# Layer 1's gate row in the weights' stream, low parts ahead of the last half sums, another order at the passage

## The chip, the cores and the metric

The kernel runs on one core of one Trainium2 chip. The metric is the device time of one execution in microseconds (us); lower is better. TensorE does the matmuls, VectorE and ScalarE the elementwise work, GpSimd (POOL) some additions and the transfers that accumulate, SyncE (SP) issues the other transfers.

## The reference, cut to what matters

One step of a backbone of two layers on 512 latent and 128 context tokens (640 in all), width 1024. Layer 0 mixes with attention and spatial gating, layer 1 with a pooling mixer. Behind each mixer stands a squared-ReLU MLP of width 4096, each sub-layer with a norm, a shift and a scale in front and a gate behind:

```python
x = x + g1 * mix
h = rms_norm(x, norm2_g[l]) * (1 + sc2) + sh2
x = x + g2 * squared_relu_mlp(h, w_ff1[l], w_ff2[l])
```

`squared_relu_mlp(h, w1, w2)` is `relu(h @ w1)**2 @ w2`. The shift, scale and gate rows come from a product of the conditioning vector with `w_mod`; latent and context tokens have rows of their own. The end is `rms_norm(x, final_g)`. Inputs and outputs are float32.

## The kernel before, in words

**Numbers.** Every large product is made of three matmuls in a fast float32 format: each operand is split into a high part (a rounding copy) and a low part (the rest), and high*high, high*low and low*high are summed (`mm3`, L823 to L825).

**Weights.** `Weights` is one stream of items in a fixed order. An item's loads go from SP into raw buffers (tag `raw`, five of them, `RAWB`); `pump` takes the next item: ScalarE makes the high part (L213), and either VectorE the low part by a subtraction (L223, `st.lo = vec`) or ScalarE a negated copy (L216) onto which GpSimd's queue adds the raw weight by an accumulating transfer (L220, `st.lo = None`). The result takes one of eight slots until `free`. With `lagging` set, the low part and the return of the raw buffer are put off to the next pump, to `lows` or to the item's use. Items with a `use` of their own make something else of the raw buffer. `caps` changes the number of raw buffers that loads may hold from a given item on.

**The order of work** is written by hand: what is issued to an engine's queue is done in that order. Generators (`bg`, `g0`, `g1`) yield after small steps, and `bg.step`, `TURNS` and `MID` say where they go on. A character of `TURNS` is one step: `0` is one step of `g0` (norm and h of the first token chunk of layer 1's MLP), `1` one of `g1` (the second chunk's pooling: norm, `hh`, windows, differences), `w` a pump with an accumulated low part, any other letter a pump with VectorE's low part. Entry 0 comes ahead of the MLP, entries 1 to 8 ahead of the eight input blocks of its first four column products (L1481 with L1786), entries 9 to 16 ahead of the squared ReLU of columns 0 to 7 (L1803).

**The passage from layer 0 to 1.** The last two blocks of layer 0's W2 run over the output columns d for both token chunks (L1835 to L1855); for the second chunk the pooling of the first (`pool_vec(0)`) goes on beside it. At d = 6 `tick0` makes the pool products of the first chunk (`pool_mm`, L2094), whose sums go into x (L1429) and are squared by ScalarE and added by VectorE (L729) for the norm of the first chunk (L740 to L684). Four pumps stand within these pool products and one behind each column from d = 6 on. Then layer 1's MLP begins with four columns at once for the first chunk (L823 to L825, `up_ps`); at column 6 the pool products of the second chunk follow. PSUM has six banks for all of these.

**Layer 1's MLP** takes blocks of 512 hidden columns. From block 2 on the up products of both chunks are made with seven half products instead of eight (`up7`, L1595): products 0 to 6 use half sums of weights (`w1s_use`, L576 to L583) and of h. The down products then have tokens on the output's rows (`down_t`, L1510), and their sums are kept per token tile t and column half q in the place of x, which was parked in memory as xT.

**The last block (b = 7).** `up7` runs for two pairs of hidden tiles; before the second, `gate_load` loads the row of the gate for the latent tokens (`G`, a raw buffer, L1691, L2020). In the second pair, `last_gate` (L2032) multiplies the kept sums of tiles 3, 2, 0 and 1 by the gate and adds the parked x by an accumulating transfer of GpSimd (L2033). Then come the down products in the order `LASTS` = 4, 3, 2, 0, 1: four halves start with two of four hidden tiles (`cut`), and are finished in turn. Tile 4 (context tokens) is summed (L1738), then gated with the second gate row (`gate_load(1)`); every other half is gated out of PSUM (L2042), added (L2043), squared by ScalarE (L2057) and multiplied by the final gain (L2059). `last_out` (L2061) makes the norm's factor, scales and stores, for the first three tiles together, then for tile 0 and tile 1; the last half of tile 1 is cut in two quarters (`TAIL`).

## Time and profile before

| what | us |
|---|---|
| median of 3 runs (lowest, highest) | 1285.55 (1285.2, 1286.9) |
| the profiled execution's own time | 1285.38 |
| its span, first to last instruction | 1283.6 |
| TensorE busy | 1247.0 (97%) |
| VectorE busy | 796.9 (62%) |
| ScalarE busy | 571.1 (44%) |
| GpSimd busy | 198.5 (15%) |
| mean granted TensorE clock | 0.988 |

The span is taken from the profiled execution; its own time is 1.8 us longer. All times in the rows below count from the span's start. In a row of a timeline the first number is the start and the second how long the instruction (or the group of so many in a row) took; consecutive instructions of one engine overlap a little, so that the distance between two starts in a full queue is shorter than the first one's time. What stands in brackets is the time that the engine stood idle before it and what ended that. PE is TensorE, DVE VectorE, ACT ScalarE. A granted clock of 1.00 is 2.4 GHz, 0.50 is 1.2 GHz.

### The profile page before, as it was taken

The numbers are of one execution on the slowest core, as the hardware profiler recorded it, in microseconds if no ns is written. First come the engines' busy times: TensorE is split into PE (matmuls) and PEld (weight loads), VectorE is DVE, ScalarE is ACT, GpSimd is POOL, SyncE is SP. The second block draws the span as 40 slices with busy tenths as digits, with TensorE's granted clock in tenths as the row PEclk, the third lists the DMA queues.
The fourth block names the chain that finished last, engine by engine and source line by source line (L and its number), as shares of the span: only waits on it lengthen the run. The fifth ranks groups of instructions, "written<-read, shape, count | busy, mean of one in ns | idle before, by whom it ended". The sixth has DMA issues, their size and how long they took to land. (4 is left out here: it accounts for less than half of the span.)

```text
span 1283.6 us, 19571 instructions
## 1 busy us (share of the span) xinstructions
PE 1247.0 (97%) x7744; PEld 1135.7 (88%) x7744; DVE 796.9 (62%) x1455; ACT 571.1 (44%) x1022; POOL 198.5 (15%) x181
## 2 busy tenths in 40 slices
PE   6999999999999999999999999899999999999986
PEld 4899975689999999999999999889898989989875
DVE  5753854554766566666666637775576556675667
ACT  4445654543554434334332424745444515445154
POOL 0010122212122221313131314210000000000030
PEclk9999999999999999999999999899999999999988
DMA  7752696250344443535353441904113343132273
GB/s 297 262 167 68 152 254 235 97 197 1 120 139 139 124 154 119 158 121 159 120 161 118 142 139 29 234 27 128 60 33 100 83 82 96 37 122 76 66 128 102
DMA packets 79163, 161.89 MB, mean 126 GB/s; under 512 B 7728, under 2 KB 34864, under 8 KB 78560
## 3 DMA queue, kind: packets, MB, share of 16 engines
q1 hardware_dynamic: 69296, 145.94, 35.6%
q0 software_dynamic: 9344, 14.35, 6.2%
q8 instruction: 61, 1.00, 0.3%
q10 hardware_dynamic: 432, 0.35, 0.1%
q14 instruction: 30, 0.25, 0.1%
HBM read 149.46 MB, written 8.02 MB: 123 GB/s over the span
## 5 line engine op out<-in xcount | busy, mean ns | idle before, releaser
L823 PE MATMUL up_ps<-h,w 128*128 128x320 f32 (+2 forms) x800 | 251.8, 315 | 4.7 <-DVE r L1632 3.1
L824 PE MATMUL up_ps<-h,w 128*128 128x320 f32 (+2 forms) x800 | 249.4, 312 | 1.2 <-DVE h L774 1.2
L825 PE MATMUL up_ps<-h,w 128*128 128x320 f32 (+2 forms) x800 | 249.9, 312 | 0.0
L213 ACT ACTIVATE w<-raw 128x1024 fp32r<-128x1024 f32 (+4 forms) x131 | 132.8, 1027 | 109.6 <-DMA raw<-w_ff 84.1
L223 DVE TENSOR_TENSOR w<-raw,w 128x1024 fp32r<-128x1024 f32 (+4 forms) x122 | 151.5, 1249 | 48.0 <-ACT w L213 47.1
L823 PEld LDWEIGHTS up_ps<-h,w 128*128 128x128 f32 x800 | 152.4, 190 | 9.1 <-issue 6.7
L823 PE MATMUL dn_ps<-aa,w 128*128 128x328 f32 (+1 forms) x512 | 159.1, 311 | 0.0
L824 PE MATMUL dn_ps<-aa,w 128*128 128x328 f32 (+1 forms) x512 | 159.0, 311 | 0.0
L825 PE MATMUL dn_ps<-aa,w 128*128 128x328 f32 (+1 forms) x512 | 158.1, 309 | 0.0
L824 PEld LDWEIGHTS up_ps<-h,w 128*128 128x128 f32 x800 | 152.7, 191 | 1.9 <-DVE h L774 1.6
L825 PEld LDWEIGHTS up_ps<-h,w 128*128 128x128 f32 x800 | 152.2, 190 | 0.3 <-DMA w<-w_ff 0.3
L484 POOL TENSOR_TENSOR acc<-acc,raw 128x1024 f32<-128x1024 f32 x42 | 100.7, 2397 | 303.7 <-ACT raw L482 303.7
L824 PE MATMUL dn_ps<-w,aa 128*128 128x512 f32 (+1 forms) x324 | 126.1, 389 | 2.4 <-DVE w L223 2.4
L823 PE MATMUL dn_ps<-w,aa 128*128 128x512 f32 (+1 forms) x324 | 126.8, 391 | 0.0
L825 PE MATMUL dn_ps<-w,aa 128*128 128x512 f32 (+1 forms) x324 | 126.3, 390 | 0.0
L1429 DVE SCALAR_TENSOR_TENSOR x<-dn_ps,mod,x 128x328 f32<-128x328 f32 (+2 forms) x168 | 67.3, 435 | 68.0 <-PE dn_ps L825 67.3
L576 ACT ACTIVATE w<-raw 128x512 fp32r<-128x512 f32 x84 | 51.0, 625 | 120.5 <-DVE raw L583 120.5
L823 PEld LDWEIGHTS dn_ps<-aa,w 128*128 128x128 f32 x512 | 96.4, 188 | 1.8 <-ACT r L1502 0.8
L825 PEld LDWEIGHTS dn_ps<-aa,w 128*128 128x128 f32 x512 | 96.3, 188 | 0.0
L824 PEld LDWEIGHTS dn_ps<-aa,w 128*128 128x128 f32 x512 | 96.2, 188 | 0.1
L482 ACT ACTIVATE raw<-raw,cs 128x1024 f32<-128x1024 f32 x42 | 48.3, 1150 | 62.5 <-DVE acc L477 58.0
L824 PEld LDWEIGHTS dn_ps<-w,aa 128*128 128x128 f32 x324 | 61.3, 189 | 15.5 <-DVE w L223 2.8
(403 smaller groups left out, 2421.1 us busy)
## 6 DMA issues: line engine op xcount, KB each, us to landing
raw<-w_ff SPq DMA_DIRECT2D x126, 512.0 KB, 3.8
raw<-w_mod SPq DMA_DIRECT2D x80, 512.0 KB, 3.9
raw<-w_m SPq DMA_DIRECT2D x16, 512.0 KB, 6.5
raw<-w_out SPq DMA_DIRECT2D x8, 512.0 KB, 4.5
w<-w_ff POOLq DMA_DIRECT2D x8, 512.0 KB, 9.8
kT<-ckvT POOLq DMA_DIRECT2D x4, 768.0 KB, 11.0
xr<-x SPq DMA_DIRECT2D x5, 512.0 KB, 6.2
xs<-x SPq DMA_DIRECT2D x2, 1280.0 KB, 10.1
```

The source lines that it names most:

```text
L213: self.nc.scalar.activation(out=hi, in_=r, func=AF.Copy)
L223: lambda: eng.tensor_tensor(out=lo, in0=r, in1=hi.bitcast(F32), op=ALU.subtract)
L482: act(out=raw if k else acc[1], in_=raw, func=AF.Copy, scale=w[1])
L484: nc.gpsimd.tensor_tensor(out=acc[1], in0=acc[1], in1=raw, op=ALU.add)
L576: act(out=w[:, 0], in_=src, func=AF.Copy)
L823: mm(ps, lhsT=st_[0], rhs=mv[0], start=first, stop=False, skip_group_check=on)
L824: mm(ps, lhsT=st_[0], rhs=mv[1], start=False, stop=False, skip_group_check=on)
L825: mm(ps, lhsT=st_[1], rhs=mv[0], start=False, stop=last, skip_group_check=on)
L1429: vec.scalar_tensor_tensor(out=xv, in0=ps[:, p0:p0 + c1 - c0], scalar=gate[:, d, m:m + 1], in1=xv, op0=ALU.mult, op1=ALU.add)
```

## The change

It has four parts. The gate row is an item of the weights' stream, ahead of the last block's W2 items, and keeps its raw buffer. In the last block the tiles come in the order `ENDS` = 3, 2, 4, 0, 1; two tiles are gated within `up7`, the other three behind the start of the down products; all five go the same way (`last_more`, `last_sq`); the low parts that are still put off are made ahead of the down products. Layer 0's W2 blocks 6 and 7 are loaded as four halves each, freed half by half, and four pumps stand at d = 3 (two), 4 and 5 instead of within the pool products and behind d = 6 and 7. `TURNS` is another, with a letter `l` for `lows`, and `lagging` is on from the start of layer 1.

```diff
--- before.py
+++ after.py
@@ -45,6 +45,7 @@
 POOL_AT = 6
 H512 = slice(0, 512)
 TAIL = slice(0, 256), slice(256, 512)
+ENDS = 3, 2, 4, 0, 1
 PARKS = 0, 1, 4, 3, 2
 PARK_AT = {(0, 4): 1, (0, 5): 1, (0, 6): 1, (0, 7): 1, (1, 4): 1, (1, 5): 2, (1, 6): 2, (1, 7): 1}
 MID = {6: (2, 1, 0, 3)}
@@ -53,7 +54,7 @@
 LAST_N = 6
 LAST_K = (4, 5)
 STEPS = (4,) * 8
-TURNS = '11w', 'w', '10', 'w01', '0w1', '01110', '11W11', '1', 'w0101', 'w1', '', '1', '', '11111', '111', '', '0w'
+TURNS = '11', '', '01', '0w', '01W', '0W1', '011', '0W1', 'l11', '11', '11', '11', '1', '11111', '111', '', '0w'
 VM_LAG = 3, 4
 AHEAD = (4, 4), (1, 1, 1, 1, 1, 1, 2)
 SPLIT = 3
@@ -596,7 +597,10 @@
                 st.add(key, [] if i else src, 0, w1s_use(l, b, p, i))
                 st.keep[key] = 2 if i == 6 else 0
 
+    halves = set()
+
     def add_w2h(l, b):
+        halves.add((l, b))
         for i in range(4):
             for k, h in [(i // 2 * 2, i % 2) if b == NFB - 1 else (i % 2 * 2, i // 2)]:
                 st.add(("w2", l, b, k, h), [(rows(a["w_ff2"][l], b * FB + k, 2, h * 512, 512), (2, 512))], 1024)
@@ -606,13 +610,14 @@
             r = (b * FB + k) * 128
             st.add(("w2", l, b, k), [(a["w_ff2"][l, r:r + 128, :], (1024,))], 1024)
 
+    grow = dr.tile([2, D], F32, name="grow")
     add_w1(0, 0)
     vm = vmods(1)
     for b in range(1, NFB + 1):
         n0 = len(st.items)
         if b < NFB:
             add_w1(0, b)
-        add_w2(0, b - 1)
+        (add_w2h if b > NFB - 2 else add_w2)(0, b - 1)
         ws, st.items[n0:] = st.items[n0:], []
         for i, w in enumerate(ws):
             st.items.append(w)
@@ -625,6 +630,10 @@
     for b in range(NFB):
         if b >= 2:
             add_w1s(1, b)
+        if b == NFB - 1:
+
+            st.add(("gate",), [(grow[0:1, :].to_broadcast([128, D]), (D,))], 0, lambda ts: cell.update({("G", 0): ts[0]}))
+            st.keep["gate",] = 0
         add_w2h(1, b)
 
 
@@ -1530,7 +1539,7 @@
             if first:
                 ps = bank("dn_ps", c[1] - c[0])
             for j, k in enumerate(ks):
-                if seven:
+                if (l, b) in halves:
                     w, v = st.need(("w2", l, b, k - k % 2, d // 4)), k % 2 * 4 + d % 4
                 else:
                     w, v = st.need(("w2", l, b, k)), d
@@ -1594,7 +1603,7 @@
 
         def up7(b, p, last=False):
             n = C[0][1]
-            gates = [(t, q) for t in LASTS[1:] for q in range(2)] if last else []
+            gates = [(t, q) for t in ENDS[0:2] for q in range(2)] if last else []
 
             def more(k=1):
                 for t, q in gates[0:k]:
@@ -1650,7 +1659,7 @@
             p1 = new("p1")
             act(out=p1, in_=pa, func=AF.Copy)
             pd = product(1, 2, None, True)
-            st.pump()
+            st.pump(1 + last)
             pb = product(2, 1, None, True)
             u2, u3 = new("u2"), new("u3")
             add(u2, p1, pb)
@@ -1687,8 +1696,6 @@
             for b in range(NFB):
                 if b >= f0:
                     for p in range(FB // 2):
-                        if b == NFB - 1 and p:
-                            gate_load(0, rawp.tile([128, 1024], F32, tag="raw", name="G"))
                         up7(b, p, b == NFB - 1 and p == 1)
 
                 cut = (lambda todo: {i: down_t(b, *i, H512, None, False, (0, 1)) for i in todo})
@@ -1718,8 +1725,9 @@
                         bg.drain()
                     continue
 
-                todo = [(t, q) for t in LASTS for q in range(2)]
-                st.pump(4)
+                todo = [(t, q) for t in ENDS for q in range(2)]
+                st.pump(5)
+                st.lows()
                 early = cut(todo[0:4])
                 w = st.slots.take([128, 2, 1024], F32)[1]
                 gate_load(1, w[:, 0])
@@ -1728,25 +1736,18 @@
                 st.slots.free += cell["spare"]
                 zs += [st.slots.take([128, 2, 1024], F32)[1].rearrange("p a n -> p (a n)") for _ in range(2)]
                 cell["zs"] = [z[:, 0:1024] for z in zs]
+                last_gate(NT - 1)
+                last_gate(ENDS[3])
+                last_gate(ENDS[4])
                 for t, q in todo:
-                    i = LASTS.index(t)
+                    i = ENDS.index(t)
                     for v in TAIL if (t, q) == todo[-1] else (H512,):
                         ps = early.pop((t, q), None)
                         ps = down_t(b, t, q, v, ps, True, range(FB) if ps is None else (3, 2))
-                        if not i:
-                            y = tile_q(t, q)
-                            vec.tensor_tensor(out=y, in0=cols(ps), in1=y, op=ALU.add)
-                            last_gate(t, (q,))
-                        else:
-                            last_more(t, q, v, ps)
-                            last_sq(t, q, v, q + (v.start > 0))
-                    if q and i == 2:
-
-                        for k in range(2):
-                            last_sq(LASTS[0], k, H512, k)
-                        last_out(LASTS[0:3], False)
-                    elif q and i > 2:
-                        last_out(LASTS[i:i + 1], i == 4)
+                        last_more(t, q, v, ps)
+                        last_sq(t, q, v, q + (v.start > 0))
+                    if q and i >= 2:
+                        last_out(ENDS[0:3] if i == 2 else ENDS[i:i + 1], i == 4)
 
         spare = []
 
@@ -1842,16 +1843,17 @@
                             if c is C[0]:
                                 st.pump()
                         if c is C[1] and d0 + n == KD:
-                            for k in range(FB):
-                                st.free(("w2", l, f2, k))
+                            free2(f2, 1)
                         tick(c, d0)
                         for d in range(d0, d0 + n):
                             residual(down(f2 + 1, d, c, pss[d - d0]), d, c, modc[l, 5])
+                            if c is C[1] and d == 3:
+                                free2(f2, 0)
+                                free2(f2 + 1, 0)
                             per_d(c, d)
                         d0 += n
                     per_c(c)
-                for k in range(FB):
-                    st.free(("w2", l, f2 + 1, k))
+                free2(f2 + 1, 1)
                 return
             if f2 < NFB - 1:
                 for d in range(KD):
@@ -2047,7 +2049,7 @@
         k = slice(v.start // 128, v.stop // 128)
         y = tile_q(t, q)[:, k]
         if (t, "ss") not in cell:
-            i3 = LASTS.index(t)
+            i3 = ENDS.index(t)
             if ("ss", i3 // 3) not in cell:
                 cell["ss", i3 // 3] = sc.tile([128, 8], F32, tag="m", name=f"ss{t}", bufs=10)
             cell[t, "ss"] = cell["ss", i3 // 3][:, i3 % 3 * 2:]
@@ -2059,7 +2061,7 @@
         vec.tensor_tensor(out=cols(cell[t, "z"][:, u]), in0=y, in1=cols(cell["fg"][:, u]), op=ALU.mult)
 
     def last_out(ts, both):
-        i3, n = LASTS.index(ts[0]), len(ts)
+        i3, n = ENDS.index(ts[0]), len(ts)
         ss = cell["ss", i3 // 3]
         i3 %= 3
         sm = sc.tile([128, 8], F32, tag="m", name=f"sm{ts[0]}", bufs=10)[:, 0:n]
@@ -2080,7 +2082,6 @@
                 eng.dma_start(out=a["y"][tok(t), u], in_=y)
 
     xT = dr.tile([T, D], F32, name="xT")
-    grow = dr.tile([2, D], F32, name="grow")
     LASTS = (4, 3, 2, 0, 1)
 
     def pool_mm(ci, N, gs=POOL_ORDER):
@@ -2097,8 +2098,6 @@
                     )
                 residual(ps, 2 * g + m, c, modc[1, 2, "p"], lambda c0: pcol(ci, c0) - p0)
                 N.square(2 * g + m)
-                if ci == 0 and m:
-                    st.pump()
 
     N = {}
     wp = {}
@@ -2119,8 +2118,7 @@
         bg.drain()
         st.flush()
         keep()
-        st.lo = None
-        st.caps["w1", 1, 0, 0] = RAWB
+        st.caps["w1", 1, 0, 2] = RAWB
         N[0] = Norm(x, C1[0], vec)
         pool_mm(0, N[0])
         bg.add(g0)
@@ -2134,8 +2132,9 @@
         norms[c].square(d)
         if c == C0[1]:
             bg.step(3)
-            if d >= POOL_AT:
-                st.pump()
+            if 3 <= d < POOL_AT:
+                st.lo = None
+                st.pump(2 if d == 3 else 1)
 
     def per_c0(c):
         if c == C0[0]:
@@ -2156,13 +2155,16 @@
 
 
         for t in what:
-            if t in "01":
+            if t == "l":
+                st.lows()
+            elif t in "01":
                 next((g0, g1)[int(t)], None)
             else:
                 st.lo = None if t == "w" else vec
                 st.pump()
                 st.lo = vec
 
+    st.lagging = True
     turn1(TURNS[0])
 
     def mid1(i):
```

## Rows read from the trace of the kernel before

**Rows 1.** TensorE's waits from 600 us on, with releaser: total us, times, longest.
```profile
PE up_ps L823 <- DVE r L1632: 3.1, 1, 3.1
...
PE dn_ps L824 <- DVE w L223: 2.4, 1, 2.4
```

**Rows 2.** TensorE's timeline, last stage: start, us; in brackets, idle before it.
```profile
1234.09 0.60 PE L823 MATMUL up_ps<-h,w 128*128 128x320 f32 x1 [3.11 <-DVE r L1632]
...
1250.10 0.50 PE L824 MATMUL dn_ps<-w,aa 128*128 128x512 f32 x1 [2.42 <-DVE w L223]
...
1272.07 0.28 PE L825 MATMUL dn_ps<-w,aa 128*128 128x256 f32 x1
```

**Rows 3.** The timeline of VectorE in the last stage.
```profile
1228.35 0.49 DVE L1632 TENSOR_TENSOR u<-u,up_ps 128x320 f32<-128x320 f32 x1
...
1231.64 1.29 DVE L2032 TENSOR_TENSOR x<-x,G 128x512 f32<-128x512 f32 x2 [2.81 <-DMA G<-grow]
...
1233.46 0.48 DVE L1632 TENSOR_TENSOR r<-u,up_ps 128x320 f32<-128x320 f32 x1
...
1236.59 1.29 DVE L2032 TENSOR_TENSOR x<-x,G 128x512 f32<-128x512 f32 x2
1237.80 1.22 DVE L223 TENSOR_TENSOR w<-raw,w 128x1024 fp32r<-128x1024 f32 x1
1238.93 0.48 DVE L1644 TENSOR_TENSOR aa<-r,aa 128x320 fp32r<-128x320 f32 x1
1239.34 0.48 DVE L1632 TENSOR_TENSOR r<-u,up_ps 128x320 f32<-128x320 f32 x1
...
1271.41 0.15 DVE L2067 TENSOR_REDUCE sm<-ss 128x1 f32<-128x2 f32 x1 [0.97 <-ACT sqy L2057]
...
1272.68 0.69 DVE L2042 TENSOR_TENSOR gy<-dn_ps,G 128x512 f32<-128x512 f32 x1
...
1274.74 0.42 DVE L2042 TENSOR_TENSOR gy<-dn_ps,G 128x256 f32<-128x256 f32 x1
...
1276.08 0.42 DVE L2042 TENSOR_TENSOR gy<-dn_ps,G 128x256 f32<-128x256 f32 x1
...
1277.00 0.42 DVE L2059 TENSOR_TENSOR w<-x,w 128x256 f32<-128x256 f32 x1
```

**Rows 4.** The timeline of ScalarE in the last stage.
```profile
1238.09 1.04 ACT L213 ACTIVATE w<-raw 128x1024 fp32r<-128x1024 f32 x1
...
1239.85 0.47 ACT L1637 ACTIVATE r<-r 128x320 f32<-128x320 f32 x1 [0.71 <-DVE r L1632]
```

**Rows 5.** The last stage's transfers: GpSimd's timeline, then issues with median us to landing.
```profile
1232.96 10.47 POOL L2033 DMA_DIRECT2D x<-xT  x8 [380.77 <-DVE x L2032]
...
x<-xT POOLq DMA_DIRECT2D x10, 256.0 KB, 10.6
...
w<-grow SPq DMA_DIRECT2D x1, 512.0 KB, 6.9
```

**Rows 6.** Two stretches: us, PE, PEld, DVE, ACT, POOL busy (count), clock, DMA share, GB/s.
```profile
809.37:846.65 37.28, 36.32 (x212) 34.12 (x212) 28.26 (x61) 24.72 (x48) 4.91 (x5) 0.91 0.71 165
...
1234.09:1240.20 6.11, 6.11 (x23) 6.11 (x24) 6.11 (x10) 4.96 (x9) 6.11 (x6) 0.50 0.88 209
```

**Rows 7.** The timelines of TensorE and VectorE at the passage from layer 0 to 1.
```profile
803.70 1.50 PE L740 MATMUL R_ps<-ones,sq 128*128 128x1 f32 x12 [1.46 <-DVE sq L729]
...
806.21 1.73 DVE L666 TENSOR_TENSOR nrm5t<-nrm5y,nrm5v 128x3 f32<-128x3 f32 x1
...
808.45 0.88 PE L684 MATMUL R_ps<-ident,nrm5y 128*128 128x128 f32 x6 [1.42 <-DVE nrm5y L668]
...
846.65 4.17 DVE L1429 SCALAR_TENSOR_TENSOR x<-pool_ps,gp,x 128x192 f32<-128x192 f32 x14
```

**Rows 8.** The groups by line at the passage: VectorE, then ScalarE, 809 to 847 us.
```profile
L774 DVE SCALAR_TENSOR_TENSOR h<-ht,mod,h 128x320 fp32r<-128x320 f32 x8 | 4.4, 548 | 3.7 <-ACT h L770 3.7
...
L216 ACT ACTIVATE w<-w 128x1024 fp32r<-128x1024 f32 x4 | 4.2, 1058 | 0.1
```

## The prediction, before the changed kernel ran

> **What bounds the kernel now.** I read four views, in this order. The waits of TensorE show where the engine that is busy for 97% of the span still stands still: of its waits behind 600 us the two longest, 3.1 and 2.4 us, lie in the last MLP block [rows 1]. The timelines say what each is [rows 2, 3]. The first: the fifth half product of the last pair must not write its bank before VectorE's sum at 1233.46 has read it, and that sum stands in VectorE's queue behind a gate product, which waited 2.81 us for the row G of the gate; G's load was issued late because its raw buffer was one of the weights' own. The second, at 1250.10: the low part of the last W2 weight (L223) stands behind the work on tile 4. The first leaves TensorE at the granted clock 0.50 (1.2 GHz) for a while: 23 matmuls took 6.11 us behind it [rows 6]. The end is a chain of VectorE, ScalarE and a store: the last product of VectorE begins at 1277.00 and ends at 1277.42, and the span ends 6.2 us later [rows 3].
>
> At the passage from layer 0 to layer 1 TensorE waits 1.46 and 1.42 us for the norm of the first chunk [rows 7]. Behind that, VectorE carries the stretch: from the first h at 809.37 to its first pool residual at 846.65 it is busy for 28.26 of 37.28 us, and 3.7 us of what is left are waits for ScalarE's h, which stands behind weight copies [rows 6 to 8].
>
> The sum goes against the profiled execution: span 1283.6, its own time 1285.38 us, 0.17 below the median of the three runs shown, 1285.55.
>
> **Part 1, the last block.** G now comes in the weights' stream, in front of the block's W2 items, some 20 us before it is used; it holds one of five raw buffers from there. One more W2 load than before therefore waits for the buffers of the last half sums, but it is used only about 10 us later: cost nothing, and about 4 us if that cover were gone. I lay VectorE's queue out anew, with the distances between the starts of rows 3: two gate halves 1.21, a weight's low part 1.13, a small sum or an aa low part 0.41. The half-size low part of the last half sum (about 0.6, half of 1.13) now comes ahead of the two u sums, which end at 1228.84; they end at 1229.45, and TensorE, which waits for the second, loses 0.6. Then tile 3's gates to 1230.65, and the sum that TensorE waited for is done at 1231.05 instead of 1233.87: the 3.1 us wait is gone. Tile 2's gates, two low parts, two sums and one aa low part follow to 1235.8. ScalarE sets the pace there: three steps of 0.5, a high copy of 1.04, six steps of 0.5 [rows 4] from 1233.8 on end at 1239.3; the last aa low part and the last W2 low part, which no longer waits for tile 4's sums, end at 1240.9. TensorE needs that one only for the second half of its second column block, after four half sums: its 2.4 us wait is gone too.
>
> Tiles 4, 0 and 1 now get their gates here, in one piece: 3 × 1.21, to 1244.5. From there VectorE works without a hole: ten halves of gate, add and product with the gain. A half takes 2.06 (1272.68 to 1274.74), a quarter 1.34 [rows 3]; the norm of the first three tiles about 1.5 and that of tile 0 1.27 behind a wait of 0.97 [rows 3]. Sum: 6 × 2.06 + 1.5 + 2 × 2.06 + 2.24 + 2.06 + 2 × 1.34 = 25.0, so the last product ends at 1269.5 instead of 1277.42: **−7.9 us**. In that are two operations more than before, one per half of tile 4 (gate, gate again, add, product; before: add, gate, product); what goes are the holes in which VectorE waited for G and for TensorE. TensorE can't be what ends last: it loses at least 3.11 + 2.42 + 3.0 (half of 6.11 at the slow clock) less 0.6, so it ends by 1264.4 instead of 1272.35 [rows 2, 6], and VectorE's last quarter begins at 1268.2. So what was a wait of TensorE becomes a queue of VectorE, and of the ten or so us that TensorE gains two stay there. Bounds of this term: −10 (VectorE as quick as TensorE) and −3 (VectorE stands for a late row or a late accumulate).
>
> The transfers that this rests on: the eight accumulates of before took GpSimd 10.47 us to issue and landed 10.6 us after their issue (median) [rows 5]. Now four go out by 1236 and six from 1241 on, 1.3 apart; the one for tile 4 should land by 1252.5 and is read at about 1253; tiles 0 and 1 have 3 us or more in hand. The row of gate 1 took 6.9 us to land [rows 5]; issued at about 1231.5, when its slot comes free, it is there by 1238.5 and used at 1240.9. SP has nothing else there but the two W2 loads.
>
> **Part 2, the passage.** Eight weights (W1 of blocks 0 and 1) used to get their low parts by a copy on ScalarE and an accumulate of GpSimd: a pair of 1.04 + 1.06 on ScalarE each [rows 4, 8], four within the pool products and four in the turns. Now four come ahead of the pool products, at d = 3 to 5 (that is why W2 of blocks 6 and 7 is split in halves and freed early), one in the turns, and three get a high copy on ScalarE and a low part on VectorE: VectorE gains 3 × 1.13 = 3.4 us of work, ScalarE loses 3 × 1.06. With the pool's squares no longer between weight copies, I lay out the queues from d = 3 on: the four pairs end at about 797, the sum of squares is ready 0.8 us sooner, so 0.7 of the 1.46 remains; the root's chain then has ScalarE free. In it one operation on 128x3 numbers took 1.73 us [rows 7], against 0.15 for one on 128x1 in rows 3; if it takes 0.2 now, the first h starts 2.65 us sooner. I take that, since GpSimd's addition of a square, which ran beside it, comes about 1 us ahead of it in my layout.
>
> Then the stretch itself: 37.28 us of VectorE becomes longer by 3.4 and shorter by the waits for h. Those do not all go: with h first, ScalarE does the 16 hh copies later, and VectorE waits for a high copy and for the first relu instead. Laid out operation by operation, the idle time falls by 0.6 only. Net: −2.65 + 3.4 − 0.6 = **+0.2 us**. TensorE begins the layer earlier and at full clock, but has six banks; the squared relus and pool residuals that free them stand in VectorE's queue among the windows, so it waits there, late in the first eight columns and in the pool products, for what it had gained. Bounds: −6 (the two waits, and about 3 us from the slow clock: a mean of 0.91 over 37.28 us [rows 6] is 6.7 us at half rate) and +4.7 (3.4 + 1.3).
>
> The rest costs nothing: the splitting of W2 keeps bytes and matmuls, and later low parts (lagging from the start of layer 1) hide behind TensorE's columns; without that cover, 0.5 us per weight.
>
> Sum: −7.9 + 0.2 = −7.7; 1285.38 − 7.7 = 1277.7, with the 0.17 to the median **1277.8**. Against no change a measurement of this kernel tells about 0.2%, 2.6 us: faster means below 1283.0, slower above 1288.1.
>
> **Rivals.** B: the passage stays bound by TensorE, my layout of VectorE being too pessimistic; then its gain of about 5 stays and the time is 1285.5 − 7.9 − 5 = 1272.6. For it: TensorE's busy share, 36.32 of 37.28 [rows 6]. Against: 28.26 + 3.4 of VectorE in a stretch that would shrink to 32, with waits of its own. C: in the last stage VectorE stands for gate 1's row or an accumulate by 4 to 5 us: 1282. For it: landing times up to 10.6 us [rows 5] and a lead of 2 and 0.5 us in my layout; against: four of the accumulates now go ahead of the others. D, slower: at the passage TensorE, waiting four times for banks, falls to 1.2 GHz as it did behind a wait of 3.1 us [rows 6], and stays there through the pool products: some 16 us of its work take twice as long, 7 of it fall into the waits, +9; with a start that is no earlier (+2.65) that is +11.7 + 0.2 − 7.9 = +4.0, 1289.5. It decides from a loss of 7.9 at the passage on. Against: the waits of 1.46 and 1.42 are as long and cost only 3 us of slow clock. F: the operation of 1.73 us [rows 7] meets GpSimd's addition again, so that the first h starts only 2.65 − 1.35 = 1.3 us sooner: 1279.1. For it: it happened before; against: GpSimd is done sooner, having no accumulates to issue there. The Trainium skill (SBUF — State Buffer, section "SBUF: two separate sides") has a rule for this: a GpSimd operation and a VectorE operation with two SBUF inputs take one port pair as a lock, and the loser waits out the other. The 1.73 us in the trace agrees with it.
>
> E: the change doesn't do what it says: G's or the low part's place in the queues is not what holds TensorE, a later wait takes over, 1285.
>
> **Chances.** Forecast 0.43, F 0.12, B 0.22, C 0.14, D 0.05, E 0.04. Forecast and F span 1275 to 1280.5 (2.5 us of doubt on waits either way); 8 in 10 need most of B and of C: 1272.0 to 1282.5. Below 1283.0 lie the forecast, F, B and most of C: 0.87; E and the rest of C within 0.2%: 0.08; slower 0.05.
>
> **What would show it.** Right: no wait of TensorE at up_ps or dn_ps over 1 us in the last block; G landed long before its first product; VectorE without holes over 0.5 us from about 1229 to the last product; TensorE's last matmul 4 us or more ahead of VectorE's last. At the passage: the wait of 1.46 halved, the first up product 2.5 us sooner, then new waits of TensorE for banks (relu sums, pool residuals), and the second chunk's first up product about where it was against the pool products' start. Wrong: the second chunk starting 4 us sooner (B), or a VectorE wait for w or xT among the last ten halves (C).

## The result, and the profile after

The median of five executions is 1277.41 us (lowest 1276.95, highest 1281.61), against 1285.2 (1280.88 to 1286.9) for five executions of the kernel before; the ratio is 0.9949, with a 95% interval of 0.9925 to 0.9973. The forecast was 1277.8. The profiled execution took 1276.95 us, its span is 1274.9.

The page, its busy times:

```profile
PE 1242.1 (97%) x7744; PEld 1132.3 (89%) x7744; DVE 799.3 (63%) x1460; ACT 569.1 (45%) x1019; POOL 195.1 (15%) x178
```

The waits of TensorE from 600 us on (total us, times, longest), its longest ones and those of the last block, where [rows 1] stood before:

```profile
PE pool_ps L2095 <- DVE r L1512: 3.1, 2, 2.0
PE up_ps L832 <- DVE r L1512: 1.0, 1, 1.0
...
PE up_ps L832 <- ACT h L779: 0.8, 1, 0.8
PE up_ps L832 <- ACT w L214: 0.8, 1, 0.8
```

The 3.1 and 2.4 us of the last block are gone, and 0.8 has come there. But waits at the passage are new, two of 3.1 us in all and one of 1.0: TensorE stands for PSUM banks that VectorE must free by its sums ahead of the squared ReLU (`r`, L1512).

The timeline of TensorE in the last stage (beside [rows 2]):

```profile
1229.51 0.39 PE L832 MATMUL up_ps<-w 128*128 128x320 f32 x1 [0.79 <-ACT w L214]
...
1262.13 0.28 PE L834 MATMUL dn_ps<-w,aa 128*128 128x256 f32 x1
```

The timeline of VectorE in the last stage (beside [rows 3]):

```profile
1230.48 0.48 DVE L1641 TENSOR_TENSOR r<-u,up_ps 128x320 f32<-128x320 f32 x1
...
1238.89 0.49 DVE L1653 TENSOR_TENSOR aa<-r,aa 128x320 fp32r<-128x320 f32 x1 [0.84 <-ACT aa L1648]
1239.30 1.22 DVE L224 TENSOR_TENSOR w<-raw,w 128x1024 fp32r<-128x1024 f32 x1
1240.44 1.29 DVE L2034 TENSOR_TENSOR x<-x,w 128x512 f32<-128x512 f32 x2
1241.64 2.49 DVE L2034 TENSOR_TENSOR x<-x,raw 128x512 f32<-128x512 f32 x4
1244.05 0.68 DVE L2044 TENSOR_TENSOR gy<-dn_ps,raw 128x512 f32<-128x512 f32 x1
...
1263.07 0.15 DVE L2069 TENSOR_REDUCE sm<-ss 128x1 f32<-128x2 f32 x1 [0.97 <-ACT sqy L2059]
...
1268.66 0.42 DVE L2061 TENSOR_TENSOR w<-x,w 128x256 f32<-128x256 f32 x1
```

From 1244.05 to 1268.66 VectorE has one hole of any size, 0.97, and each half takes 2.06, as laid out. TensorE's last matmul, at 1272.07 before [rows 2], begins at 1262.13, 6.5 us ahead of VectorE's last product. The bound has moved from TensorE's waits to VectorE's queue.

At the passage, TensorE and VectorE (beside [rows 7]):

```profile
805.11 1.50 PE L749 MATMUL R_ps<-ones,sq 128*128 128x1 f32 x12 [0.61 <-DVE sq L738]
...
807.29 0.16 DVE L675 TENSOR_TENSOR nrm5t<-nrm5y,nrm5v 128x3 f32<-128x3 f32 x1
...
808.28 0.78 PE L693 MATMUL R_ps<-ident,nrm5y 128*128 128x128 f32 x6
```

The wait of 1.46 became 0.61, the operation of 1.73 us takes 0.16, and the wait of 1.42 is gone.

These starts can't be compared as they stand. Up to the first pool product the two programs differ only in how the last W2 weights of layer 0 are cut and in some early pumps, for which TensorE doesn't wait, yet that product begins at 791.74 before and at 794.01 after. The windows view shows part of it at the very start. The first 40 us of the kernel before, then of the changed kernel (length, PE, PEld, DVE, ACT, POOL busy with counts, granted clock, DMA share, GB/s):

```profile
0.00:40.00 40.00, 29.43 (x218) 21.72 (x219) 24.12 (x57) 15.30 (x27) 1.12 (x10) 0.96 0.78 288
```
```profile
0.00:40.00 40.00, 30.34 (x212) 22.76 (x212) 23.17 (x53) 15.17 (x26) 1.12 (x10) 0.91 0.76 282
```

TensorE stood longer at 1.2 GHz in the second (a mean of 0.91 against 0.96; as an estimate, 0.05 × 40 = 2 us of work at full clock). So I cut each trace into four stretches at starts that both timelines show. A ends at the first pool product, B at the second chunk's first up product, C at the first down product of block 6 of layer 1, D at the end of the span. D thus holds block 6's down products and the whole last block. The clocks are the windows view's, of 0 to 40 and of 800 to 870 us; the last column is the median of the executions. The runs' names are explained in the next section.

| kernel | A | clock | B | clock | C | D | median |
|---|---|---|---|---|---|---|---|
| before | 791.74 | 0.96 | 67.82 | 0.95 | 322.21 | 101.81 | 1285.20 |
| changed | 794.01 | 0.91 | 67.62 | 0.98 | 320.32 | 92.95 | 1277.41 |
| c_after (changed) | 795.29 | 0.87 | 67.61 | 0.98 | 320.42 | 92.97 | 1277.52 |
| e1_last | 794.02 | 0.91 | 68.60 | 0.95 | 322.20 | 93.45 | 1280.49 |
| e2_passage | 793.31 | 0.91 | 67.62 | 0.98 | 320.43 | 100.86 | 1283.64 |
| e3_g_late | 792.23 | 0.91 | 68.87 | 0.95 | 320.33 | 95.90 | 1279.11 |
| e4_low_late | 794.80 | 0.87 | 69.76 | 0.90 | 321.84 | 96.19 | 1281.64 |
| e5_w | 794.95 | 0.87 | 69.48 | 0.93 | 322.14 | 93.38 | 1277.82 |
| e6_lag_later | 792.70 | 0.91 | 73.99 | 0.88 | 322.57 | 92.85 | 1283.19 |
| e7_gain_pool | 793.05 | 0.91 | 68.99 | 0.95 | 320.33 | 95.13 | 1278.43 |
| e8_norm0_later | 793.49 | 0.91 | 69.79 | 0.90 | 321.89 | 92.24 | 1276.92 |
| e9_gates_early | 792.04 | 0.91 | 68.95 | 0.95 | 320.41 | 90.91 | 1274.38 |
| e10_all | 794.06 | 0.87 | 69.10 | 0.95 | 320.41 | 89.69 | 1275.66 |
| e10_again | 791.36 | 0.96 | 69.19 | 0.95 | 320.30 | 89.71 | 1274.23 |

Column D repeats within 0.02 us where a kernel was traced twice, and is what the experiments on the last block are read by. One part of it isn't the change's: from the end of VectorE's last product to the end of the span it takes 5.8 us in ten of the traces and 6.2 in four (before, e1, e5, e7), so a difference of 0.4 in D tells nothing unless the last product moved too. B can be compared at equal clock only; A tells nothing of a change.

### The profile page after: what moved, and what is told of

Same layout as the page of the kernel before. It is cut to its first block, busy times and chain, and to the rows that moved or that the text cites. A ratio compares the mean times of both kernels' runs of the same rounds, so it can differ in the third digit from the quotient of the medians.

```text
span 1274.9 us, 19562 instructions
## 1 busy us (share of the span) xinstructions
PE 1242.1 (97%) x7744; PEld 1132.3 (89%) x7744; DVE 799.3 (63%) x1460; ACT 569.1 (45%) x1019; POOL 195.1 (15%) x178
## 5 line engine op out<-in xcount | busy, mean ns | idle before, releaser
L224 DVE TENSOR_TENSOR w<-raw,w 128x1024 fp32r<-128x1024 f32 (+4 forms) x125 | 155.1, 1248 | 46.5 <-ACT w L214 45.5
L832 PEld LDWEIGHTS up_ps<-h,w 128*128 128x128 f32 x800 | 150.8, 188 | 5.9 <-issue 3.4
L833 PEld LDWEIGHTS up_ps<-h,w 128*128 128x128 f32 x800 | 151.1, 189 | 0.7 <-DVE h L783 0.5
L834 PEld LDWEIGHTS up_ps<-h,w 128*128 128x128 f32 x800 | 150.7, 188 | 0.0
```

Source lines behind the costliest of these rows:

```text
L224: lambda: eng.tensor_tensor(out=lo, in0=r, in1=hi.bitcast(F32), op=ALU.subtract)
L832: mm(ps, lhsT=st_[0], rhs=mv[0], start=first, stop=False, skip_group_check=on)
L833: mm(ps, lhsT=st_[0], rhs=mv[1], start=False, stop=False, skip_group_check=on)
L834: mm(ps, lhsT=st_[1], rhs=mv[0], start=False, stop=last, skip_group_check=on)
```

## The experiments

**e1_last**: the new last block with the old passage. The W2 halves of layer 0, the early pumps, the turns and the lag are undone; the core of it:

```
-            if 3 <= d < POOL_AT:
-                st.lo = None
-                st.pump(2 if d == 3 else 1)
+            if d >= POOL_AT:
+                st.pump()
...
-    st.lagging = True
     turn1(TURNS[0])
```

> The kernel before with the last block of the changed kernel alone: gate row in the weights' stream, new order of tiles, low parts ahead, gates in one piece; the passage is the old one. Theory (VectorE's queue of the last block carries the whole gain, the passage is worth nothing): the last product of VectorE ends 7.9 to 8.6 us sooner than before, the time is 7.9 to 8.6 below the kernel before, so the same as the changed kernel within 1 us. Rival 1 (the passage gives 2 us, as the starts of layer 1's blocks in the two traces suggest, and a slower start of the run hid it): also 8 below the kernel before here, but the passage alone is then 2 us below it too. Rival 2 (the passage as a whole is a gain of 4 or more, TensorE-bound): this run stays 4 us above the changed kernel.

Median 1280.49 against 1284.97 (ratio 0.9959, 0.9947 to 0.9971). D fell by 8.36, in the range that the theory gave for the last product; B stayed 0.78 above the kernel before. The last block carries most of the gain. But the theory's time was missed, and so was rival 1's: the median fell by 4.5 only and lies 3.1 above the changed kernel. By the two traces 1.9 of that is stretch C, 1.0 is B (at a clock of 0.95 against 0.98) and 0.5 is D. The 3.1 is nearer to rival 2's 4 than to the theory's 1, but a gain of 4 at the passage is not what e2 shows.

**e2_passage**: the new passage with the old last block (the rest of the change's diff: its edits to `add_w2h`, `free2`, the pumps, `TURNS` and the lag).

> The kernel before with the new passage alone (halved W2 of the last two blocks of layer 0, weights ahead of the pool products, new turns, low parts later from the start of layer 1); the last block is the old one. Theory: 0.2 us above the kernel before, within 1 us of it; the second chunk's first up product stands where it did, counted from the pool products' start. Rival 1 (the 0.7 us wait of the second chunk and small gains in every block are the change's own): 2 us below the kernel before, with the seconds chunk's third column block 1 us sooner than in the kernel before. Rival 2 (TensorE-bound passage): 4 or more below.

Median 1283.64 (ratio 0.9984, 0.9967 to 1.0001), 1.3 below the kernel before, which the noise covers. B is 67.62 (67.82 before, at a lower clock), so about where it was, as the theory has it; C is 1.8 shorter, as rival 1 has it, so the theory's term of nothing for the rest fell; in the old last block the waits of 3.1 and 2.4 us stand where they stood:

```profile
1233.41 0.61 PE L826 MATMUL up_ps<-h,w 128*128 128x320 f32 x1 [3.09 <-DVE r L1635]
...
1249.21 0.69 PE L827 MATMUL dn_ps<-w,aa 128*128 128x512 f32 x1 [2.42 <-DVE w L223]
```

**e3_g_late**: G loaded as in the kernel before, all else as changed (the one extra pump that took the gate's item goes with it).

```
-            st.add(("gate",), [(grow[0:1, :].to_broadcast([128, D]), (D,))], 0, lambda ts: cell.update({("G", 0): ts[0]}))
...
+                        if b == NFB - 1 and p:
+                            gate_load(0, rawp.tile([128, 1024], F32, tag="raw", name="G"))
```

> The changed kernel with the row G loaded as in the kernel before (at the last pair of the last block, into a raw buffer that the weights must first give back) and not in the weights' stream; all else as changed. Theory (from the last up products on VectorE and ScalarE form one queue without slack): VectorE waits some 2.8 us for G with the half sum behind it, TensorE's 3.1 us wait is back, and the end comes 2.8 to 3.1 us later than in the changed kernel. Rival 1 (TensorE sets the end): wait and slow clock both count, 3.1 + 3.0 = 6 us later. Rival 2 (the early low part and the order of the gates do it all, G is covered): 0.

D is 2.95 longer than in the changed kernel (median +1.7). VectorE's wait for G is back, with the sum behind it:

```profile
1230.88 1.29 DVE L2032 TENSOR_TENSOR x<-x,G 128x512 f32<-128x512 f32 x2 [2.65 <-DMA G<-grow]
1232.70 0.48 DVE L1637 TENSOR_TENSOR r<-u,up_ps 128x320 f32<-128x320 f32 x1
```

That is the theory's size and not the 6 of rival 1. TensorE waited 2.93 us and its last matmul came 5.2 us later within the stretch, but the end came only 2.95 later: TensorE's wait and its slow clock cost nothing beyond VectorE's own hole.

**e4_low_late**: no low parts ahead of the half sums.

```
                 st.pump(5)
-                st.lows()
                 early = cut(todo[0:4])
```

> The changed kernel without the low parts ahead of the half sums: the low part of the last W2 weight comes when TensorE first asks for it, which puts it in VectorE's queue behind the gates of tiles 4, 0 and 1 and the first half's three products. Theory (VectorE's queue sets the end): TensorE waits about 4.5 us in its second column block, but VectorE loses only the hole that this makes in its queue, 1.8 us by my layout, so 1.8 us above the changed kernel, and TensorE's last matmul comes 4 to 6 us later than in it. Rival 1 (TensorE sets the end, as a wait of 2.4 us stood in the kernel before): 4.5 us and a share of slow clock, +5 to +6. Rival 2 (there is room for the low part anywhere): 0.

TensorE waited 4.15 us, and its last matmul came 6 us later within the stretch; D grew by 3.24. VectorE's timeline shows where that is:

```profile
1249.42 1.22 DVE L224 TENSOR_TENSOR w<-raw,w 128x1024 fp32r<-128x1024 f32 x1
1253.02 0.69 DVE L2043 TENSOR_TENSOR gy<-dn_ps,raw 128x512 f32<-128x512 f32 x1 [2.38 <-PE dn_ps L834]
...
1262.01 0.69 DVE L2043 TENSOR_TENSOR gy<-dn_ps,w 128x512 f32<-128x512 f32 x1 [0.57 <-PE dn_ps L834]
```

Two holes, 2.38 + 0.57 = 2.95, are most of the loss. I had laid out 1.8; that the slow clock makes up the difference is likely but was not tested. Behind the wait TensorE ran at a mean granted clock of 0.54:

```profile
1250.70:1254.40 3.70, 3.70 (x9) 2.94 (x10) 1.34 (x2) 0.00 (x0) 1.80 (x2) 0.54 1.40 175
```

**e5_w**: three low parts back to GpSimd's accumulate.

```
-TURNS = '11', '', '01', '0w', '01W', '0W1', '011', '0W1', 'l11', '11', '11', '11', '1', '11111', '111', '', '0w'
+TURNS = '11', '', '01', '0w', '01w', '0w1', '011', '0w1', 'l11', '11', '11', '11', '1', '11111', '111', '', '0w'
```

> The changed kernel with the three low parts of the turns that VectorE makes given back to the accumulate of GpSimd (a second copy on ScalarE, 3 x 1.06, and a transfer), so 3.4 us less on VectorE and 3.2 more on ScalarE at the passage. Theory (VectorE's queue of residuals, windows and low parts sets the passage; TensorE's bank waits of 1.0, 3.1 and 0.3 us are its sign): the bank waits shrink by 2 to 3 us in total, the second chunk's first up product comes 1 to 2.5 us sooner after the pool products' start than the 67.6 of the changed kernel. Rival 1 (ScalarE, which makes h, relu and the copies, sets it as well): what VectorE gains comes back as waits for h, 0 to +1. Rival 2 (TensorE-bound): no change in either place.

Median 1277.82, no difference from the changed kernel that can be told; B is 69.48 at a clock of 0.93. None of the three has the mechanism. The bank waits vanished, as the theory wanted, but TensorE now waits for the accumulates themselves (waits at the passage, 803 to 872 us):

```profile
PE up_ps L834 <- DMA w<-w_ff: 5.7, 3, 2.8
```

They land 9.3 us after their issue (median), and the weights are wanted before. Sparing these waits is what VectorE's 3.4 us of added work at the passage buy.

**e6_lag_later**: the lag only from the end of the first chunk on, as before.

```
-    st.lagging = True
     turn1(TURNS[0])
```

> The changed kernel with the low parts of the turns issued at once again and not one item later (the switch stays where it was in the kernel before, at the first chunk's end). Theory: within 0.5 us of the changed kernel at the second chunk's start, and the 1.1 us that the stretch from there to the first half sums gains, and 0.75 us over the four blocks behind, stay, as they come from where the weights' stream stands and not from this switch. Rival 1: the switch is what moves the relu sum that TensorE waited 0.7 us for; then both gains are gone, +1.9. Rival 2 (the switch lets h lead VectorE's queue): the first h columns wait for low parts, 1.2 us each, +1 to +3 at the passage.

Median 1283.19, 5.8 above the changed kernel. The theory fell: B is 73.99, some 5 us longer than the 68.9 to 69.2 at clock 0.95 (part of it is a lower clock, 0.88), with these waits of TensorE (803 to 872 us):

```profile
PE up_ps L832 <- DVE r L1512: 3.5, 2, 2.1
PE pool_ps L2095 <- DVE r L1512: 2.0, 1, 2.0
PE up_ps L833 <- DVE h L783: 1.1, 1, 1.1
```

Why the banks come free late can be read from VectorE's waits of the same 69 us, first in this run, then in the changed kernel:

```profile
DVE w L224 <- ACT w L214: 6.3, 3, 3.2
```
```profile
DVE w L224 <- ACT w L214: 1.6, 2, 1.2
```

VectorE stands 4.7 us longer for ScalarE's high copies before it can make the three low parts, and its sums and h stand behind them. That is rival 2's direction, with more than its 1 to 3 us.

And the 0.7 us wait of the second chunk is back, as rival 1 said, while the four blocks behind keep what they gained, which rival 1 denied. The same mechanism can be read in the kernel before, VectorE in the second chunk:

```profile
878.69 1.23 DVE L223 TENSOR_TENSOR w<-raw,w 128x1024 fp32r<-128x1024 f32 x1 [0.46 <-ACT w L213]
879.84 0.48 DVE L1503 TENSOR_TENSOR r<-r,up_ps 128x320 f32<-128x320 f32 x1
880.85 0.49 DVE L1506 TENSOR_TENSOR aa<-r,aa 128x320 fp32r<-128x320 f32 x1 [0.54 <-ACT aa L1505]
881.81 1.23 DVE L223 TENSOR_TENSOR w<-raw,w 128x1024 fp32r<-128x1024 f32 x1 [0.46 <-ACT w L213]
```

A round lasts 3.12 us: VectorE waits for ScalarE's high copy before it makes the low part, and the next sum, which frees TensorE's bank, stands behind both. One item later, the same place in the changed kernel:

```profile
880.53 0.48 DVE L1512 TENSOR_TENSOR r<-r,up_ps 128x320 f32<-128x320 f32 x1
881.55 0.49 DVE L1515 TENSOR_TENSOR aa<-r,aa 128x320 fp32r<-128x320 f32 x1 [0.54 <-ACT aa L1514]
881.96 1.22 DVE L224 TENSOR_TENSOR w<-raw,w 128x1024 fp32r<-128x1024 f32 x1
883.09 0.48 DVE L1512 TENSOR_TENSOR r<-r,up_ps 128x320 f32<-128x320 f32 x1
```

The copy is done by then; a round lasts 2.56 us.

**e7_gain_pool**: four of the products with the gain on GpSimd.

```
+        eng = nc.gpsimd if ENDS.index(t) < 2 else vec
-        vec.tensor_tensor(out=cols(cell[t, "z"][:, u]), in0=y, in1=cols(cell["fg"][:, u]), op=ALU.mult)
+        eng.tensor_tensor(out=cols(cell[t, "z"][:, u]), in0=y, in1=cols(cell["fg"][:, u]), op=ALU.mult)
```

> The changed kernel with the product with the gain of the first two tiles of the last stage (four products of 128x512, 0.69 us each on VectorE with a pitch of 0.72) on GpSimd, which is idle there but for the last accumulates. Theory (VectorE's queue sets the end, TensorE is done 6 us ahead): VectorE's last product comes up to 4 x 0.69 = 2.8 us sooner, if GpSimd's product does not hold VectorE up. Rival 1 (the port lock, by the rule of the Trainium skill, SBUF — State Buffer, section SBUF: two separate sides: a VectorE operation with two SBUF operands waits out GpSimd's): each GpSimd product of some 1.4 us, estimated from its 128x312 additions of 0.85 to 1.0, holds one VectorE addition for up to that time, 0 to +2.8. Rival 2 (TensorE sets the end): 0.

Rival 1 came true. D is 2.18 longer, and the last product 1.8 later in it (the rest is the 6.2 us at the end). GpSimd, then VectorE:

```profile
1246.36 9.05 POOL L2062 TENSOR_TENSOR z<-x,w 128x512 f32<-128x512 f32 x4
```
```profile
1246.52 1.67 DVE L2045 TENSOR_TENSOR x<-gy,x 128x512 f32<-128x512 f32 x1
1248.12 0.68 DVE L2044 TENSOR_TENSOR gy<-dn_ps,raw 128x512 f32<-128x512 f32 x1
1248.83 1.28 DVE L2045 TENSOR_TENSOR x<-gy,x 128x512 f32<-128x512 f32 x1
...
1250.75 2.29 DVE L2045 TENSOR_TENSOR x<-gy,x 128x512 f32<-128x512 f32 x1
...
1253.68 2.30 DVE L2045 TENSOR_TENSOR x<-gy,x 128x512 f32<-128x512 f32 x1
```

Four additions took 7.54 instead of 2.76 us, 4.8 more, against the 2.9 that the four products gave; the product that reads PSUM stayed at 0.68. That agrees with the Trainium skill (SBUF — State Buffer, section "SBUF: two separate sides"): the lock holds a VectorE operation with two SBUF inputs, and `gy`, with one input in PSUM, isn't one.

**e8_norm0_later**: the norm of the last tile but one, behind the first half of the last.

```
-                    if q and i >= 2:
-                        last_out(ENDS[0:3] if i == 2 else ENDS[i:i + 1], i == 4)
+                    if q and i == 2:
+                        last_out(ENDS[0:3], False)
+                    elif i == 4:
+                        last_out(ENDS[3 + q:4 + q], q)
```

> The changed kernel with the norm and output of the last tile but one put behind the first half of the last tile, so that VectorE does not stand for ScalarE's squares (0.97 us idle ahead of that norm in the changed kernel). Theory (VectorE's queue sets the end): the last product comes 0.9 to 1.2 us sooner, the time is 0.9 to 1.2 below the changed kernel. Rival 1: ScalarE's scalings of that tile now stand in front of the last squares and give it back, 0. Rival 2 (TensorE or the stores set the end): 0.

D is 0.71 shorter, less than the theory's 0.9 and more than the rivals' nothing: the 0.97 is gone, and a wait of 0.37 for the buffer of ScalarE's squares has come, since the squares still stand behind six scalings. The median, 1276.92, is 0.5 below the changed kernel, which alone would tell nothing.

**c_after**: the changed kernel again, beside the next two.

> The changed kernel once more, beside the next two. All theories: 1277.4 within the spread of its runs. From the trace: the stretch from the first half sums of the last chunk of layer 1 (after the up products of its second half) to the end within 0.3 us of the first trace of the changed kernel; the start of the run, up to the pool products, may lie anywhere between 791.7 and 795, as it did in the traces so far although nothing is changed there.

Median 1277.52 against 1284.38 (ratio 0.9948, 0.9934 to 0.9963); D within 0.02 of the first trace, A at 795.3.

**e9_gates_early**: G ahead of the last block's W1, its eight gates where VectorE waits 4.67 us for TensorE.

```
+            if b == NFB - 1 and not p:
+                for t in ENDS[0:2] + ENDS[3:]:
+                    last_gate(t)
...
-                last_gate(ENDS[3])
-                last_gate(ENDS[4])
```

> The changed kernel with the row G one place earlier in the weights' stream (ahead of the last block's W1) and the gate products of the four tiles that use it (8 of 128x512, pitch 0.6 us, 4.8 us in all) at the start of the last block, where VectorE waits 4.67 us for TensorE. Theory (behind the up products VectorE is one queue without slack, so each microsecond of work taken out of it ends 1 us sooner, until TensorE's sums come last): the four gates of tiles 0 and 1 (2.4 us) leave the queue ahead of the first product, which is then bound by TensorE's sum, 1.9 us sooner; so 1.9 to 2.5 us below the changed kernel. Rival 1 (the accumulate of tile 4, issued at 1241.7 and landing 8.8 us later, becomes what VectorE waits for): 0.5 to 1 less of it. Rival 2 (G takes a raw buffer from the last block's W1 and TensorE waits for weights): 0 or slower by up to 2. Rival 3 (TensorE sets the end): 0.

Median 1274.38 against 1284.38 (ratio 0.9924, 0.991 to 0.9939); D is 2.04 shorter than the changed kernel's, and no rival's wait (an accumulate, a weight) is seen. The hole in the changed kernel, then the same place here, where eight gates fill it and the first product follows the two gates of tile 4 at once:

```profile
1214.74 0.49 DVE L1641 TENSOR_TENSOR u<-p,up_ps 128x320 f32<-128x320 f32 x1 [4.67 <-PE up_ps L834]
```
```profile
1209.44 4.90 DVE L2035 TENSOR_TENSOR x<-x,raw 128x512 f32<-128x512 f32 x8
1214.26 0.48 DVE L1644 TENSOR_TENSOR u<-p,up_ps 128x320 f32<-128x320 f32 x1
...
1240.26 1.29 DVE L2035 TENSOR_TENSOR x<-x,w 128x512 f32<-128x512 f32 x2
1241.46 0.69 DVE L2045 TENSOR_TENSOR gy<-dn_ps,raw 128x512 f32<-128x512 f32 x1
```

**e10_all**: the same with the later norm of e8 and the scalings of the first three tiles put between the squares, one tile's two behind each.

```
                         last_sq(t, q, v, q + (v.start > 0))
+                        for f in cell.get("todo", [])[0:1]:
+                            f()
+                        cell["todo"] = cell.get("todo", [])[1:]
...
+        if n > 1:
+            scale(0, ts[0])
+            cell["todo"] = [lambda i=i: scale(i, ts[i]) for i in range(1, n)]
```

> The run with the early gates, and also the norm of the last tile but one behind the first half of the last tile, and ScalarE's six scalings of the first three tiles put two by two between the squares, so that no square stands behind them. Theory: 0.7 (what the later norm gave by itself) + 0.4 (the wait for ScalarE's squares that it had left) below the run with the early gates, so 3 us below the changed kernel in all. Rival (the queue is bound by TensorE's sums once the gates are gone): the same as the run with the early gates.

D is 89.69, so 3.26 below the changed kernel and 1.2 below e9, as the theory has it. Its median, 1275.66, is 1.3 above e9's, with an A of 794.06 against 792.04. Hence once more:

**e10_again**: no edit.

> The run with early gates, later norm and interleaved scalings once more, as it is. By its trace it took 3.3 us less than the changed kernel from the last block's start on, and 1.2 less than the run with the early gates alone, while its median was 1.3 above that run's. Theory (the median carries the start of the run and the passage, which differ between executions of the same code by 2 to 3 us): from the last block's start to the end within 0.3 us of 89.7 again, the median anywhere from 1272.5 to 1276. Rival (the later norm or the interleaved scalings cost something outside of the traced run): again 1.3 above the run with early gates alone, so 1275.3 to 1276.3.

D is 89.71 and the median 1274.23 (1271.38 to 1279.34; ratio 0.9935, 0.9914 to 0.9957). So the theory's first half holds, and the rival's 1275.3 or more was not seen. Both e9 and e10 beat the changed kernel (c_after, 1277.52); between the two the medians tell nothing, and only the traces' stretch D does.

## Why the prediction was right, and where a step was not

- **The 3.1 us wait, G in the stream.** Right. e3 puts its worth at 2.95, as VectorE's hole and not as TensorE's wait with its clock.
- **The 2.4 us wait, low parts ahead.** Right; e4 loses 3.24 without them. TensorE's wait at the half-size low part is 0.79 where 0.19 stood before, so 0.60 more, as laid out. (The profile names ScalarE's copy as what ended it, the prediction VectorE's second u sum; the two ended within 0.1 us of each other.)
- **VectorE's tail without a hole, 25.0 us, last product at 1269.5.** Right. It ended at 1269.08, from 1244.05 on in 25.03, behind TensorE by 6.5 us. By itself the last block gave 8.4 us with the old passage (e1 against the kernel before) and 7.9 with the new one (the changed kernel against e2), the forecast being 7.9. The 8.86 between the two D of before and after holds more than that: 0.4 is the store's end, and about 0.6 comes with the new passage, as e2 has it too. The prediction's own sign, no hole over 0.5 us, was set too strictly: there are two, the 0.84 in the stretch where it has ScalarE set the pace, and the 0.97 that its sum contains. That VectorE is the bound is shown from both sides: e9 takes 2.4 us of work out of the queue and gains 2.04, e8 takes out a hole of 0.97 and gains 0.71. Rival C fell: no wait for a row or an accumulate stands among the ten halves; the accumulates landed 8.8 us after issue (median).
- **The first h 2.65 sooner.** Right: from the first pool product to the first `ht` it was 17.63 us (791.74 to 809.37) and is 15.09 (794.01 to 809.10). The 1.73 us operation stands in both traces with the old passage (the kernel before and e1_last) and is 0.16 in all twelve with the new one, so rival F fell. In the kernel before, GpSimd's addition of a square, 806.57 to 807.90, ends as that operation does, at 807.94; in the changed kernel it is over at 807.12, before that operation begins at 807.29. What holds the operation was not tested further.
- **The passage +0.2.** Not contradicted, within what can be told. In the two traces the first h comes 2.54 sooner and the stretch from it to the first pool residual is 2.3 longer (39.62 instead of 37.28), laid out as −2.65 and +2.8. At equal clock (0.95) B was 67.82 and 68.60 with the old passage, and is 68.87 to 69.19 with the new one where nothing else of it is changed: 0.3 to 1.4 longer, with only two traces of the old one, which differ by 0.8 themselves. The new waits for banks are where they were laid out, and VectorE is busy for 31.48 us of the stretch (28.26 before, [rows 6]): 3.2 more, laid out as 3.4:

```profile
809.10:848.72 39.62, 35.09 (x213) 32.37 (x213) 31.48 (x64) 22.61 (x45) 1.30 (x2) 0.96 0.35 89
```

Rivals B and D fell. No gain of 5 stayed. And the clock behind the waits, which in the runs with this passage unaltered was 0.90 to 0.98 from 800 to 870 us, costs far less than D's 11.7: at 0.90 (e4, e8) B and C together are 391.6 to 391.7 us, at 0.98 387.9 to 388.1, so 3.7 us lie between the two.
- **"The rest costs nothing" is the step that failed**, as a term of the sum sized at 0. It gave 1.9 us: stretch C is 320.3 to 320.4 in the runs with the new passage and a clock of 0.95 or more, and 322.2 in both runs with the old one. About 1.1 lies ahead of the first down product of block 2, where the wait of 0.7 stood (e6 brings that wait back by the lag alone). The 0.75 over the four blocks behind lies in their down products: these took 27.36 to 27.61 us a block before and in e1, and 27.23 to 27.24 in the changed kernel, with TensorE busy throughout at a clock of 1.00 in both. So it is their pace and no wait, and its cause stays open. And the lag is not just something that costs nothing under the cover of TensorE's columns: the new passage needs it. Without it, in e6, the passage loses some 5 us, and VectorE's added wait of 4.7 us for three weights is 1.6 each, against the 0.5 per weight that the prediction named.

The forecast's total is nearer than its terms, and that is luck. The two traces give D −8.9, C −1.9, B −0.2 and A +2.3, together −8.7; A isn't the change's. Without A, and with B at equal clock (+0.3 to +1.4), 9.4 to 10.5 us should be seen, and the medians differ by 7.8 and 6.9. So the 1.9 us that the forecast left out were hidden by a gap of 1.6 to 3.6 us. What the executions of the kernel before that were not traced did in A and in D (where its trace has 1.2 GHz behind two waits) isn't known, so that gap stays open. The twenty executions of the kernel before that ran beside e1 to e4 lie between 1279.81 us, at a mean granted clock of 0.992, and 1288.45, at 0.986.

## What to carry to other kernels

Where an engine's wait has its cause in another engine's queue, lay out that queue operation by operation up to the end of the kernel: the wait's own length and the clock behind it may cost nothing, as in e3, and the queue's holes are the sum. Once the queue is the bound, look for the last stretch in which its engine is idle and move whole operations there; in e9 the eight gate products cost nothing in a hole of 4.67 us at the start of the last block. Where an operation follows another engine's copy at once, try to issue it one item late, so that the queue behind it doesn't stand for the copy (e6).

## What was not expected of the hardware

- Nearly the same code, up to the first pool product, took from 791.36 to 795.29 us in fourteen traces, roughly in step with the granted clock of the first 40 us (0.96: 791.4 and 791.7; 0.91: 792.0 to 794.0; 0.87: 794.1 to 795.3). With differences of 1 us, compare a stretch and not the end.
- Four GpSimd products of 128x512 took 9.05 us in all beside VectorE's additions, and stretched these from 0.69 to up to 2.30 us each. The products' records overlap (2.3 to 4.9 us each, the first while accumulates were still being issued), so whether one takes the 1.4 us that I had estimated from smaller additions no run shows.
- An accumulate into SBUF of 512 KB from GpSimd's queue landed 9.3 to 11.5 us after its issue (the medians of the fourteen traces), so that three of them, issued in the turns, cost TensorE 5.7 us of waits in e5_w.
